# A two-layer fp32 encoder whose instruction order is made with the scheduler's other simulated clock

## The chip, the cores and the metric

The kernel runs on one core of a Trainium2 chip. The metric is the device time of one execution in microseconds (us). The kernel before was run three times: 2852.09, 2852.01 and 2848.87 us, median 2852.01 us. A second set of numbers comes from one execution under the hardware profiler.

## The reference, cut to what matters

Two requests of 512 and 256 tokens, 768 rows in all, share the weights. D is 1024, the hidden width of a feed-forward network (FFN) is 2816, everything is fp32.

```python
def swiglu_ffn(x, w1, w2):
    gate, up = jnp.split(x @ w1, 2, axis=-1)
    return (jax.nn.silu(gate) * up) @ w2
...
# one layer; DEPTH is 2: layer 0 has the HGRN2 mixer, layer 1 windowed attention
x = x + 0.5 * swiglu_ffn(rmsnorm(x, g0), w1a, w2a)
x = x + mixer(rmsnorm(x, g1))
x = x + 0.5 * swiglu_ffn(rmsnorm(x, g2), w1b, w2b)
...
y = rmsnorm(x, final_g)
```

The HGRN2 mixer is a gated linear recurrence in both directions over 8 heads of width 128 (`S_t = diag(f_t) S_{t-1} + k_t v_t^T`). The attention mixer has 16 query and 4 key heads of width 64, a window of 128 tokens to either side, rotary positions on part of a head, and a sink logit for each head.

## The kernel before, in words

**Arithmetic.** Every fp32 operand of a large product is split in two fp32r parts, hi by a cast on ACT and lo by a subtraction on DVE. A product is then three matmuls on PE (hi by hi, hi by lo, lo by hi: `mm3`, lines 261 to 263). Weights are loaded by SP (`load_next`), split by `plain_steps` (lines 166 and 167) or by `quad_steps` (lines 199 and 200), and stand in 8 buffers `w`. There are 8 PSUM banks (`ps`) and 21 large slots (`big`).

**The FFNs** (f0 to f3, one before and one after each mixer) multiply in a Strassen-Winograd form, 7 products p1 to p7 in place of 8. `up_pair` makes a gate tile and an up tile (matmuls on line 421, evacuations on lines 438 to 455). After every four such pairs `down_quad` multiplies by w2: in the order p1, p2, p5, p4, p7, p6, p3 (`DOWN`), each product three banks of 6 matmuls with 512 columns (line 479). A bank of p1 is first added to the residual x (line 501, DVE), then p2 accumulates into the same bank and is added again; p4 does so upon p5, p3 upon p7. So the first matmul of p2 waits for DVE's addition of p1, and the first of p4 for that of p5. This change from up to down happens five times in each FFN, 20 times in all.

**The HGRN mixer.** `hgrn_proj` projects the next head (lines 261 to 263, evacuated on line 654) while `hgrn_scan` goes through the seven levels of a head's scan. A level is six 128 by 128 matmuls (line 671; the trace shows 12 records for them), whose result DVE copies under a mask (line 690); then DVE multiplies q by the level's decay (line 713) and ACT copies the next level's k operand (line 696). The next level's matmuls read that q and that operand, so a level can't start until the one before has gone through DVE. `weave` sets pieces of the next head's projection between the levels.

**The attention mixer.** A unit is a group of four query heads by one block of 128 queries (24 units). `turn` transposes q (line 910) and ACT copies it out (line 1097); `scores` multiplies by k (lines 1106, 1107); then exponentials, a multiplication on POOL (line 1138), the transposes of the probabilities (line 1144), the products with v (lines 1156, 1157), and the split of the outcome (lines 983, 984). `pipeline` sorts all these calls by a step number, with the pieces of the q projection and of the output projection as further events.

**The start and the end.** `load_x` normalizes the first three blocks (lines 303 to 306), turns them (line 323), then starts f0; `up_plain` makes the first tiles (lines 412, 413). `final_block` normalizes and stores each block (lines 1030 to 1037) as soon as f3 has added to it.

**What sets the order.** No engine's order is written out by hand. The code's own order gives each instruction a priority; the Tile framework simulates the program, with a clock for every engine, and puts next on an engine, of the instructions that its simulated clock finds ready, the one that comes first in the code. Pools of buffers, semaphores and waits follow from that order. `kernel` makes the context in line 1277, `with _tile.TileContext(nc) as tc:`; the loops that say what is computed do not depend on it.

## Time and profile before

| | |
|---|---|
| three runs, us | 2852.09, 2852.01, 2848.87 |
| the profiled execution's own time, us | 2852.12 |
| its span in the trace, us | 2850.3 |
| PE busy, us | 2796.7 (98%) |
| DVE busy, us | 2173.2 (76%) |
| ACT busy, us | 1318.9 (46%) |
| POOL busy, us | 355.1 (12%) |

The page gives busy times by engine and the costliest groups; the windows view gives busy times of a stretch, with the clock that was granted to PE; the waits view gives, for each line, how long an engine stood idle and what ended it; the timeline gives single instructions. The stages lie so: the start up to 28 us, f0 until about 540, HGRN until about 1080, f1 and f2 until about 2060, attention until about 2350, f3 and the final norm to the end. An engine carries out its instructions in order, so an instruction that waits holds up what stands behind it.

### The profile page before, as it was taken

What the parts mean: (1) busy time and instruction counts of PE and PEld (TensorE: products, weight loads), DVE (VectorE), ACT (ScalarE), POOL (GpSimd) and SP (SyncE); (2) the same over time, 40 slices, a digit from 0 to 9 for tenths busy, and PEclk for the clock granted to TensorE, in tenths of its full rate; (3) what the DMA queues carried; (4) which work ended last, traced back from release to release, by engine and by line L of the source; (5) the groups of instructions that cost most, each with busy time, mean ns of one, the idle gap of its engine ahead of it and who ended that gap; (6) DMA issues with size and microseconds to landing.
All of it is one profiled execution on the core that took longest, in us unless ns stands there. A gap on an engine that the chain in (4) does not pass through costs nothing. (4 is left out here: it accounts for less than half of the span.)

```text
span 2850.3 us, 40558 instructions
## 1 busy us (share of the span) xinstructions
PE 2796.7 (98%) x15225; PEld 2554.2 (90%) x15225; DVE 2173.2 (76%) x3750; ACT 1318.9 (46%) x2454; POOL 355.1 (12%) x402
## 2 busy tenths in 40 slices
PE   8999999999999999999999999999999899999998
PEld 8899999889899889998998998999888789989997
DVE  7788787468577658878878887887848878788877
ACT  7344443434344336434444643444458755434443
POOL 1111111000000001111111111111002211111110
PEclk9999999999999999999999999999999999999999
DMA  6554454311111133555444355545422113555443
GB/s 165 127 125 122 116 134 121 115 44 39 44 39 38 60 97 86 132 127 122 123 119 114 84 134 127 122 121 124 126 71 75 37 51 90 135 126 125 117 121 96
DMA packets 330101, 291.37 MB, mean 102 GB/s; under 512 B 11608, under 2 KB 257840, under 8 KB 329904
## 3 DMA queue, kind: packets, MB, share of 16 engines
q1 hardware_dynamic: 294064, 212.43, 25.4%
q0 software_dynamic: 31680, 62.93, 12.6%
q10 hardware_dynamic: 4160, 13.42, 1.3%
q8 instruction: 119, 1.95, 0.3%
q14 instruction: 78, 0.64, 0.1%
HBM read 216.39 MB, written 9.44 MB: 79 GB/s over the span
## 5 line engine op out<-in xcount | busy, mean ns | idle before, releaser
L421 PE MATMUL ps<-big,w 128*128 128x384 f32 x6720 | 1172.8, 334 | 3.1 <-DVE tA L444 2.9
L421 PEld LDWEIGHTS ps<-big,w 128*128 128x128 f32 x6720 | 1165.4, 188 | 8.8 <-DVE tA L444 7.2
L199 ACT CAST w<-wr 128x512 fp32r<-128x512 f32 x600 | 416.1, 707 | 722.7 <-PE ps L421 321.0
L479 PE MATMUL ps<-w,big 128*128 128x512 f32 x2520 | 586.8, 391 | 17.4 <-DVE x L501 17.4
L479 PEld LDWEIGHTS ps<-w,big 128*128 128x128 f32 x2520 | 469.4, 188 | 129.7 <-DVE x L501 17.3
L200 DVE TENSOR_TENSOR w<-wr,w 128x512 fp32r<-128x512 f32 (+1 forms) x520 | 438.1, 853 | 95.7 <-ACT w L199 87.0
L501 DVE SCALAR_TENSOR_TENSOR x<-ps,x 128x512 f32<-128x512 f32 x468 | 305.5, 682 | 20.5 <-PE ps L479 10.2
L141 POOL DMA_DIRECT2D s<-wr x120 | 105.4, 878 | 1333.4 <-DMA wr<-in_ffn_w_dram 583.0
L261 PE MATMUL ps<-w,big 128*128 128x512 f32 x624 | 249.8, 400 | 0.2
L263 PE MATMUL ps<-w,big 128*128 128x512 f32 x624 | 245.2, 393 | 2.5 <-DVE big L330 1.3
L262 PE MATMUL ps<-w,big 128*128 128x512 f32 x624 | 244.4, 392 | 0.0
L266 ACT CAST big<-tA 128x384 fp32r<-128x384 f32 x296 | 148.0, 513 | 175.0 <-DVE tA L449 72.0
L261 PE MATMUL ps<-big,w 128*128 128x384 f32 (+2 forms) x640 | 220.8, 346 | 3.3 <-ACT big L266 2.0
L262 PE MATMUL ps<-big,w 128*128 128x384 f32 (+2 forms) x640 | 216.8, 339 | 0.7 <-DVE big L267 0.5
L263 PE MATMUL ps<-big,w 128*128 128x384 f32 (+2 forms) x640 | 215.7, 337 | 0.0
L167 DVE TENSOR_TENSOR w<-wr,w 128x1024 fp32r<-128x1024 f32 x92 | 111.6, 1222 | 83.6 <-ACT w L166 59.7
L141 POOL DMA_DIRECT2D wr<-wr x100 | 87.5, 875 | 680.0 <-DVE tA L350 319.8
L267 DVE TENSOR_TENSOR big<-tA,big 128x384 fp32r<-128x384 f32 x296 | 164.2, 566 | 7.9 <-ACT big L266 4.4
L206 DVE TENSOR_TENSOR wr<-wr,wr 128x512 f32<-128x512 f32 (+1 forms) x100 | 79.3, 793 | 114.5 <-DMA wr<-wr 85.9
L166 ACT CAST w<-wr 128x1024 fp32r<-128x1024 f32 x92 | 96.6, 1052 | 120.5 <-PE ps L262 99.7
L263 PEld LDWEIGHTS ps<-w,big 128*128 128x128 f32 x624 | 117.4, 188 | 28.8 <-DVE big L330 2.0
L261 PEld LDWEIGHTS ps<-w,big 128*128 128x128 f32 x624 | 117.8, 189 | 22.3 <-issue 0.6
(170 smaller groups left out, 3317.2 us busy)
## 6 DMA issues: line engine op xcount, KB each, us to landing
wr<-in_ffn_w_dram SPq DMA_DIRECT2D x264, 512.0 KB, 3.9
s<-in_ffn_w_dram SPq DMA_DIRECT2D x120, 256.0 KB, 3.0
s<-wr POOLq DMA_DIRECT2D x120, 256.0 KB, 4.0
wr<-wr POOLq DMA_DIRECT2D x80, 256.0 KB, 4.0
wr<-in_hg_w_in_dram SPq DMA_DIRECT2D x40, 512.0 KB, 3.8
wr<-wr POOLq DMA_DIRECT2D x20, 512.0 KB, 4.6
spill<-x ACTq DMA_DIRECT2D x12, 512.0 KB, 3.0
x<-spill ACTq DMA_DIRECT2D x12, 512.0 KB, 3.3
```

The lines of the kernel that those rows point to most:

```text
L141: self.nc.gpsimd.dma_start(out, src, accum_op=ALU.add)
L167: self.nc.vector.tensor_sub(lo, raw, hi.bitcast(F32))
L199: nc.scalar.copy(h, src)
L200: (eng or nc.vector).tensor_sub(l, src, h.bitcast(F32))
L261: nc.tensor.matmul(out, a[0], b[0], start=first, stop=False)
L262: nc.tensor.matmul(out, a[0], b[1], start=False, stop=False)
L263: nc.tensor.matmul(out, a[1], b[0], start=False, stop=last)
L266: self.nc.scalar.copy(hi, src)
L267: self.nc.vector.tensor_sub(lo, src, hi.bitcast(F32))
L421: self.nc.tensor.matmul(ps, a[x], b[y], start=first and k == 0 and i == 0, stop=k == 3 and i == 2, skip_group_check=True,)
L479: nc.tensor.matmul(ps, a[x], w[y], start=name == chain and kp == 0 and q == 0, stop=kp == 1 and q == 2, skip_group_check=True,)
L501: self.nc.vector.scalar_tensor_tensor(x, ps, c, x, ALU.mult, ALU.add)
```

## The change

One argument is added where the context is made. The scheduler then takes the time of its simulation from another clock, one that models the timeline of the engines and of their queues. No loop, tile, pool or instruction of the program is edited.

```diff
-    with _tile.TileContext(nc) as tc:
+    with _tile.TileContext(nc, schedule_with_timeline_sim=True) as tc:
         tile_trunk_kernel(tc, *args)
```

Each engine gets the same instructions in another order, but for three activation table loads fewer on ACT (19 for 22; two at the start, around the first use of line 412, and one where the HGRN stage begins). On PE an instruction moves 6 rows on average, at most 61 up and 32 down; on DVE 1.8 rows; POOL's order is the same, and on SP four rows at the start move.

**From up to down in an FFN, on PE (third group of f1).** `ps_11106` is the bank of the last up product p3, `ps_11239` to `ps_11255` are the three banks of p1 and p2 of the down products (weights `w_11122`, `w_11123` for p1, `w_11153`, `w_11154` for p2), `ps_11294` to `ps_11310` those of p5. Before, from the end of p1 to p5:

```order
L479 MATMUL ps_11255<-w_11123,big_10795 128x512
L479 MATMUL ps_11255<-w_11122,big_10795 128x512
L479 MATMUL ps_11239<-w_11153,big_10923 128x512
L479 MATMUL ps_11239<-w_11154,big_10923 128x512
L479 MATMUL ps_11239<-w_11153,big_10923 128x512 x2
```

Now, at the beginning of p1:

```order
L479 MATMUL ps_11239<-w_11122,big_10795 128x512 x2
L479 MATMUL ps_11239<-w_11123,big_10795 128x512
L421 MATMUL ps_11106<-big_9142,w_11064 128x384 x6
L421 MATMUL ps_11106<-big_9145,w_11064 128x384 x6
L479 MATMUL ps_11239<-w_11122,big_10795 128x512
```

And now from the end of p1 on, down to the first matmul of p2:

```order
L479 MATMUL ps_11255<-w_11122,big_10795 128x512
L479 MATMUL ps_11294<-w_11184,big_10951 128x512
L479 MATMUL ps_11294<-w_11185,big_10951 128x512
L479 MATMUL ps_11294<-w_11184,big_10951 128x512
L479 MATMUL ps_11302<-w_11184,big_10951 128x512
L479 MATMUL ps_11302<-w_11185,big_10951 128x512
L479 MATMUL ps_11302<-w_11184,big_10951 128x512
L479 MATMUL ps_11310<-w_11184,big_10951 128x512
L479 MATMUL ps_11310<-w_11185,big_10951 128x512
L479 MATMUL ps_11310<-w_11184,big_10951 128x512
L479 MATMUL ps_11239<-w_11153,big_10923 128x512
```

Five of p1's matmuls now stand ahead of the 12 of the last up product, and nine matmuls of p5 stand between p1 and p2. Further on, pieces of p7 stand between those of p2, and p4 comes after p6's first two banks. The other 19 changes from up to down read alike, but for the lengths of the pieces.

**Two levels of a scan, on PE (first head).** `ps_5321` and `ps_5322` are one level's banks, `ps_5355` and `ps_5356` the next one's; `ps_5313` and `ps_5369` are projection. Before, the level stands so, and 18 matmuls onto `ps_5313` follow before the next level comes:

```order
L262 MATMUL ps_5313<-big_4591,w_5049 128x512
L263 MATMUL ps_5313<-big_4591,w_5050 128x512
L671 MATMUL ps_5321<-big_4938,big_5151 128x128 x4
L671 MATMUL ps_5322<-big_4938,big_5151 128x128 x2
L261 MATMUL ps_5313<-big_4592,w_5049 128x512
L262 MATMUL ps_5313<-big_4592,w_5049 128x512
L263 MATMUL ps_5313<-big_4592,w_5050 128x512
```

Now:

```order
L262 MATMUL ps_5313<-big_4597,w_5049 128x512
L263 MATMUL ps_5313<-big_4597,w_5050 128x512
L671 MATMUL ps_5321<-big_4938,big_5151 128x128 x4
L671 MATMUL ps_5322<-big_4938,big_5151 128x128 x2
L671 MATMUL ps_5355<-big_4938,big_5151 128x128 x4
L671 MATMUL ps_5356<-big_4938,big_5151 128x128 x2
L261 MATMUL ps_5369<-big_4590,w_5049 128x256
```

The 18 projection matmuls have moved ahead of the first of the two levels, and nothing stands between the levels. Eight pairs of levels of the stage stand so now, one in six of the heads and two in one, and one more pair has only four matmuls between; before, the shortest piece between two levels was seven matmuls of 512 columns. On DVE the rows between two such levels are what they were: the two of line 690, line 713, then lines 719 and 717.

**A unit of attention, on PE.** `ps_18983` takes the turned queries, `tA_18988` their copy on ACT, `ps_19003` the first scores; `ps_18889` is output projection. Before:

```order
L910 MATMUL ps_18983<-ident_r,big_18955 128x128 x4
L1144 MATMUL ps_18990<-ident_r,big_18831 128x128 x4
L261 MATMUL ps_18889<-w_18809,big_17852 128x512
L262 MATMUL ps_18889<-w_18810,big_17852 128x512
L263 MATMUL ps_18889<-w_18809,big_17852 128x512
L1106 MATMUL ps_19003<-big_17939,tA_18988 128x256
```

Now:

```order
L1157 MATMUL ps_18936<-tA_18915,big_17943 128x512
L910 MATMUL ps_18983<-ident_r,big_18955 128x128 x4
L1144 MATMUL ps_18990<-ident_r,big_18831 128x128 x4
L1106 MATMUL ps_19003<-big_17939,tA_18988 128x256
L1107 MATMUL ps_19003<-big_17939,tA_18988 128x256
```

The three projection matmuls stand earlier, together with others, in pieces of 12 to 24. Between a unit's turn and its scores there are now at most four transposes of line 1144 in 16 of the 24 units; before it was so in 7.

**The start and the end.** At the start ACT casts two pieces of weights (line 166) earlier, and the table load of line 412 comes after the third square root of line 304. On DVE line 413 now stands ahead of the three of line 306; before it stood behind two of them. At the end the last 72 matmuls of f3 are mixed so that the first block is complete after 27 of them instead of 15, and DVE's last additions of line 501 stand ahead of the multiplications of line 1037.

## The prediction

> **What bounds the kernel now.** I read the page's first part, then the windows of the stages, then the waits of PE, and at last the timeline where the change moves PE's rows. The page:

> ```profile
> span 2850.3 us, 40558 instructions
> PE 2796.7 (98%) x15225; PEld 2554.2 (90%) x15225; DVE 2173.2 (76%) x3750; ACT 1318.9 (46%) x2454; POOL 355.1 (12%) x402
> ```

> PE is busy for all but 2850.3 - 2796.7 = 53.6 us. The change adds and removes no matmul, so at an unchanged pace no more than these 53.6 us can be won, and a loss shows as more of them. The windows tell where they lie (columns: length, busy time of PE, PEld, DVE, ACT, POOL with counts, granted clock, DMA share, GB/s):

> ```profile
> 0.00:50.00 50.00, 37.93 (x211) 36.56 (x212) 35.14 (x50) 39.10 (x66) 5.60 (x10) 0.97 0.67 182
> 600.00:1050.00 450.00, 449.94 (x2778) 402.33 (x2777) 303.69 (x538) 169.89 (x297) 0.00 (x0) 1.00 0.17 50
> 1100.00:2050.00 950.00, 940.00 (x4979) 877.25 (x4978) 766.78 (x1216) 416.24 (x731) 147.87 (x146) 1.00 0.49 121
> 2050.00:2350.00 300.00, 289.42 (x1549) 239.79 (x1548) 214.56 (x597) 203.73 (x513) 53.03 (x98) 0.99 0.20 61
> 2800.00:2850.00 50.00, 42.41 (x223) 39.22 (x221) 33.89 (x56) 20.10 (x38) 1.81 (x1) 0.96 0.22 84
> ```

> In HGRN (600 to 1050) PE idles 0.06 us in 450: nothing can be won there. In f1 and f2 it idles 10.0 us in 950, in attention 10.6 in 300, at the start 12.1 and at the end 7.6. PE's waits (line that waits, what ends the wait: us, times, longest):

> ```profile
> PE ps L479 <- DVE x L501: 17.4, 37, 0.5
> PE ps L910 <- DVE big L267: 3.1, 3, 1.9
> PE ps L421 <- DVE tA L444: 2.9, 5, 1.1
> PE ps L1106 <- ACT tA L1097: 2.5, 6, 1.3
> PE ps L1144 <- POOL big L1138: 2.1, 3, 1.3
> ```

> So the FFNs lose nearly all they lose in one place, where p2 and p4 wait for line 501.

> **Part 1, up to down (20 places).** One place of f1 on PE, then DVE there:

> ```profile
> 1401.79 4.28 PE L479 MATMUL ps<-w,big 128*128 128x512 f32 x18
> 1406.62 10.24 PE L479 MATMUL ps<-w,big 128*128 128x512 f32 x44 [0.54 <-DVE x L501]
> 1417.32 14.80 PE L479 MATMUL ps<-w,big 128*128 128x512 f32 x64 [0.46 <-DVE x L501]
> ...
> 1405.32 0.55 DVE L453 TENSOR_TENSOR tA<-tA,ps 128x384 f32<-128x384 f32 x1
> 1405.79 0.68 DVE L501 SCALAR_TENSOR_TENSOR x<-ps,x 128x512 f32<-128x512 f32 x1
> ```

> A matmul of 512 columns costs 14.80 / 64 = 0.23 us. p1's first bank is full 6 x 0.23 = 1.4 us after 1401.79; DVE, still at the last up product (line 453), adds it only from 1405.79 to 1406.47. p2 would start after 18 matmuls, at 1405.9, and waits until 1406.62. In the new order the last up product's 12 matmuls come five matmuls (1.15 us) later, so that line's work and the addition shift by 1.15 us, to 1407.6; the nine of p5 push p2's start by 9 x 0.23 = 2.1 us, to about 1408.0. The wait goes, with 0.4 us to spare. p4 now follows p6 and most of p7, so its wait for p5's additions should go too; a hand replay leaves between 0 and 0.27 us there. The five waits of line 421 for line 444 (2.9 us) stand at the last up product, which now comes behind five matmuls (1.15 us, the longest wait is 1.1). All of it is 17.4 + 2.9 = 20.3 us; with 20 x 0.27 = 5.4 left, 14.9. I take **-15 us**, between -20 and -8 (the margin of 0.4 us lost in half of the places, 0.54 each, and some left at p4).

> **Part 2, two scan levels back to back (HGRN).** Two consecutive levels of one head:

> ```profile
> 594.85 1.60 PE L671 MATMUL ps<-big,big 128*128 128x128 f32 x12
> 596.20 0.49 PE L261 MATMUL ps<-big,w 128*128 128x512 f32 x1
> 596.01 1.06 DVE L690 COPY_PREDICATED big<-big,ps 128x512 f32<-128x512 uint8 x2 [0.17 <-PE ps L671]
> 596.97 0.94 DVE L713 TENSOR_TENSOR big<-big,big 128x768 f32<-128x768 f32 x1
> 599.03 1.50 PE L671 MATMUL ps<-big,big 128*128 128x128 f32 x12
> 600.29 0.48 PE L261 MATMUL ps<-big,w 128*128 128x512 f32 x1
> 601.08 0.95 DVE L713 TENSOR_TENSOR big<-big,big 128x768 f32<-128x768 f32 x1
> ```

> The level begins at 594.85 and PE is at the next row at 596.20. The following level needs line 713, over at 596.97 + 0.94 = 597.91. Projection covers the 1.71 us between; for the second level it is 602.03 - 600.29 = 1.74. Where nothing stands between, PE must wait those 1.7 us, since the projection taken out has already run: PE was never idle here, so running it sooner wins nothing. Eight pairs at 1.7 make 13.6; the pair with four matmuls (0.91 us) left waits 0.8. Together **+14.4 us**. From below it is 8, if DVE reaches both lines 0.7 us earlier in a quiet stretch; from above 20, if a cast's subtraction (line 167) gets between in some.

> [...]

> ```profile
> 2232.71 0.33 PE L1144 MATMUL ps<-ident_r,big 128*128 128x128 f32 x1 [1.27 <-POOL big L1138]
> 2233.95 0.33 PE L1144 MATMUL ps<-ident_r,big 128*128 128x128 f32 x1 [0.68 <-POOL big L1138]
> 2232.00:2236.00 4.00, 2.61 (x9) 1.91 (x10) 4.00 (x11) 2.66 (x7) 1.89 (x2) 0.82 0.44 132
> 2236.00:2240.00 4.00, 2.91 (x14) 2.10 (x12) 1.72 (x3) 1.81 (x6) 0.00 (x0) 0.76 0.26 73
> ```

> After waits of 1.27 and 0.68 us in quick succession the granted clock was 0.82 and then 0.76 over 8 us. That pair cost 4 x (0.18 + 0.24) = 1.7 us on top. In HGRN each new gap stands alone, several microseconds of matmuls from the next, so I count no clock loss there and keep it as a rival.

> **Part 3, attention.** The turn, its copy and its scores:

> ```profile
> 2226.80 0.46 PE L910 MATMUL ps<-ident_r,big 128*128 128x128 f32 x4
> 2227.47 0.48 PE L261 MATMUL ps<-w,big 128*128 128x512 f32 x1
> 2227.70 0.57 ACT L1097 CAST tA<-ps 128x512 fp32r<-128x512 f32 x1
> 2228.32 0.39 PE L1106 MATMUL ps<-big,tA 128*128 128x256 f32 x1
> ```

> From the turn to the end of the copy it is 2228.27 - 2226.80 = 1.47 us, of which turn and transposes take 0.67. With the projection moved away PE waits up to 0.8 us there. This holds in 16 units instead of 7. The seven cost 2.5 us in six waits, 0.42 each; nine more at that price are +3.8, and if all 16 cost 0.8 it is 12.8 - 2.5 = +10.3. Against it, bundles of 12 to 24 matmuls elsewhere may cover the waits of lines 910 and 1144 (3.1 + 2.1): at best 3.8 - 5.2 = -1.4. I take **+5**, between -2 and +11: nearer the middle of the two, since POOL's and DVE's chains that lines 1144 and 910 wait for are not shortened.

> **Part 4, start and end.** The start:

> ```profile
> 24.22 0.75 DVE L306 TENSOR_SCALAR big<-x,stat 128x1024 f32<-128x1024 f32 x1
> 25.43 1.03 PE L323 MATMUL ps<-ident_r,big 128*128 128x128 f32 x8
> 25.13 0.49 ACT L412 ACTIVATE tA<-ps 128x384 f32<-128x384 f32 x1
> 25.64 1.28 ACT L304 ACT_TABLE_LOAD   x1
> 26.93 0.29 ACT L304 ACTIVATE stat<-stat,eps 128x1 f32<-128x1 f32 x1
> 27.13 1.98 ACT L166 CAST w<-wr 128x1024 fp32r<-128x1024 f32 x2
> 27.10 0.55 DVE L413 TENSOR_TENSOR tA<-tA,ps 128x384 f32<-128x384 f32 x1 [1.40 <-PE ps L263]
> 28.21 0.44 PE L261 MATMUL ps<-big,w 128*128 128x384 f32 x1 [1.23 <-ACT w L166]
> ```

> Two table loads fewer save ACT 2 x 1.28 = 2.6 us, and the wait of 1.23 us for line 166 should go, since that cast is earlier. But line 306, which the turns (line 323) need, now stands behind line 413 on DVE, and that one waits for line 412. ACT now has the two casts (1.98) and a third square root (0.29, the one at 26.93) ahead of line 412's table load: from 23.83, where the load began, it would begin at 26.1, and line 412 end at 26.1 + 1.28 + 0.49 = 27.9. Lines 413 and 306 take 0.55 + 0.75, so the first turn starts near 29.2. PE's other matmuls, which ended at 28.21 - 1.23 = 27.0 with eight turns (1.03) among them, are through at about 26.0: some 3 us of wait for the 1.2 that goes. The start is **+2**, between 0 and +4. At the end the first block is complete 12 matmuls (2.7 us) later, the last matmul stays where it is, and the last additions come sooner on DVE; the norms of six blocks are squeezed into less time. I take **+1.5**, between 0 and +3.

> **The sum.** -15 + 14.4 + 5 + 2 + 1.5 = +7.9 us. The profiled execution took 2852.12 us (its span and 1.8 us around it), the median of the runs is 2852.01, so nothing is to be corrected: 2852.1 + 7.9 = **2860 us**.

> **The rivals.**

> *No change.* The waits between levels are mostly shorter than 1.7 us, about 1.0 (8 + 0.4 us), and attention comes out even: -15 + 8.4 + 0 + 3.5 = -3, 2849 us. For it: the page shows DVE busy 76%, so at some of the pairs it may be ahead of where the two quoted levels caught it. Against it: on DVE the chain is 1.06 + 0.94 = 2.0 us of work however free it is.

> *Faster.* The gaps between levels don't appear at all, because the next level's q is ready when PE comes there; the rest stays: 2852.1 - 6.5 = 2845.6, say 2846 us. It decides from a price of 0.1 us a pair down (8 x 0.1 = 0.8, so that the sum passes -5.7). For it: PE's time in HGRN has been free of waits until now. Against it: both quoted levels give 1.7 us by DVE's rows alone, and DVE's order between the levels is unchanged.

> *Slower still, by the clock.* Each of the nine new gaps brings the clock down as at 2232: 9 x 1.7 = 15 us more, 2875 us. The row for it is that one alone, and it had two gaps within two microseconds. [...]

> That the order would not change is excluded: the rows shown above differ.

> **How the numbers follow.** About 0.2% (5.7 us) is what a measurement of this kernel can tell from no change. My forecast, 2860 us with its own range of 2853 to 2868, has 0.50, no change 0.26, faster 0.12, the clock 0.12. The low end of the forecast's own range, under 2857.8, I set against the high end of the no-change case above it, and leave the cases as they are: slower by over 0.2% 0.50 + 0.12 = 0.62, within 0.2% 0.26, faster 0.12. The range goes from 2845, where the faster rival lies, to 2874, just short of the clock's 2875.

> **What would show it.** Right: PE's wait for line 501 falls from 17.4 us to under 6; line 671 shows about nine waits for line 713 of 1.5 to 1.9 us, and PE idles some 14 us in the HGRN stage, which had 0.06; line 1106 waits more than 2.5 us in all; the clock stays at 1.00 in HGRN. Wrong: part 1 if line 479 still waits for line 501 over 10 us; part 2 if line 671 shows no waits, or if they are of another size; part 3 if attention's idle time falls from 10.6 us; and the whole forecast if the pace of the matmuls changes where PE doesn't wait, since all terms are waits.

## The result, and the profile after

The changed kernel takes 2884.55 us (median of 4 runs, 2882.04 to 2885.64) against 2851.95 for the kernel before (4 runs, 2848.87 to 2852.09). The ratio is 1.0116, with a 95% interval of 1.0098 to 1.0133: slower by 32.6 us, where the forecast was 8 us, and above the range's 2874. The profiled execution took 2884.88 us. Its page and its windows, in the columns of before:

```profile
span 2883.1 us, 40670 instructions
PE 2802.3 (97%) x15225; PEld 2576.1 (89%) x15225; DVE 2158.9 (75%) x3750; ACT 1315.2 (46%) x2451; POOL 369.6 (13%) x402
```

```profile
0.00:50.00 50.00, 36.52 (x194) 35.22 (x195) 28.46 (x43) 31.52 (x56) 4.53 (x9) 0.93 0.69 181
600.00:1050.00 450.00, 432.57 (x2680) 388.10 (x2679) 293.73 (x527) 164.99 (x293) 0.00 (x0) 1.00 0.16 48
1100.00:2050.00 950.00, 947.25 (x5046) 893.04 (x5046) 770.50 (x1230) 426.39 (x746) 155.75 (x146) 1.00 0.48 120
2050.00:2350.00 300.00, 269.64 (x1410) 224.54 (x1409) 199.38 (x569) 187.36 (x482) 51.76 (x96) 0.95 0.18 59
```

PE now idles 17.4 us in HGRN, where it had 0.06, and 30.4 us in the attention window, where it had 10.6; there the granted clock fell to 0.95 too. In the window of f1 and f2 its idle time went from 10.0 to 2.8 us. PE's waits:

```profile
PE ps L671 <- DVE big L713: 13.9, 8, 2.4
PE ps L1106 <- ACT tA L1097: 13.2, 11, 2.3
PE ps L111 <- DMA tB<-in_hg_g_norm_dram: 7.9, 1, 7.9
PE ps L910 <- DVE big L267: 6.6, 2, 4.2
PE ps L261 <- ACT big L266: 5.8, 4, 2.5
PE ps L671 <- ACT big L696: 4.6, 6, 1.7
PE ps L910 <- DVE stat L1134: 3.3, 1, 3.3
```

Line 479's waits for line 501, 17.4 us before, are gone, and so are those of line 421. Windows at fixed times compare different work once one kernel runs behind the other. The following table goes by work: each row is the time from the start of one matmul to the start of another in PE's timeline (FFNs: first to last of line 421, four sums; scan: first to last of line 671; attention: first of line 910 to last of line 1157; seams: what lies between). The cuts don't hold quite the same work: 27 projection matmuls of the seam behind attention now lie in the attention stretch, and six more in the scan.

| stretch, us | before | changed | difference |
|---|---|---|---|
| start, to the first up pair | 55.3 | 58.3 | +3.0 |
| the four FFNs | 1772.3 | 1737.9 | -34.4 |
| seam f0 to scan | 88.1 | 90.9 | +2.8 |
| scan | 363.5 | 384.3 | +20.8 |
| seams scan to f1, f2 to attention | 189.8 | 191.2 | +1.4 |
| seam f1 to f2 | 55.8 | 61.6 | +5.8 |
| attention | 228.7 | 263.3 | +34.5 |
| seam attention to f3 | 72.3 | 69.1 | -3.2 |
| end, from f3's last up product | 24.6 | 26.6 | +2.1 |
| span | 2850.3 | 2883.1 | +32.8 |

One change from up to down in f1, on PE:

```profile
1411.70 1.31 PE L479 MATMUL ps<-w,big 128*128 128x512 f32 x5
1412.86 2.27 PE L421 MATMUL ps<-big,w 128*128 128x384 f32 x12
1414.96 27.63 PE L479 MATMUL ps<-w,big 128*128 128x512 f32 x121
1442.43 37.80 PE L421 MATMUL ps<-big,w 128*128 128x384 f32 x217
```

No wait stands in it: 121 matmuls run through at 27.63 / 121 = 0.228 us. Two scan levels back to back, PE and then DVE:

```profile
607.79 1.50 PE L671 MATMUL ps<-big,big 128*128 128x128 f32 x12
610.93 1.58 PE L671 MATMUL ps<-big,big 128*128 128x128 f32 x12 [1.63 <-DVE big L713]
...
608.88 1.05 DVE L690 COPY_PREDICATED big<-big,ps 128x512 f32<-128x512 uint8 x2 [1.02 <-PE ps L671]
609.83 0.95 DVE L713 TENSOR_TENSOR big<-big,big 128x768 f32<-128x768 f32 x1
```

This is the wait that was forecast, 1.63 us for 1.7: line 713 ends at 610.78, and the level starts 0.15 later. A unit of attention, PE and ACT, and the window that follows:

```profile
2180.70 0.46 PE L910 MATMUL ps<-ident_r,big 128*128 128x128 f32 x4
2180.99 0.62 PE L1144 MATMUL ps<-ident_r,big 128*128 128x128 f32 x4
2183.70 0.39 PE L1106 MATMUL ps<-big,tA 128*128 128x256 f32 x1 [2.08 <-ACT tA L1097]
...
2181.99 0.51 ACT L1122 ACTIVATE big<-big,stat 128x256 f32<-128x256 f32 x1
2182.49 0.50 ACT L1122 ACTIVATE big<-big,stat 128x256 f32<-128x256 f32 x1
2183.07 0.57 ACT L1097 CAST tA<-ps 128x512 fp32r<-128x512 f32 x1
```

```profile
2183.90:2187.50 3.60, 3.60 (x15) 3.13 (x15) 3.30 (x15) 2.61 (x9) 1.71 (x4) 0.53 0.01 3
2201.00:2204.60 3.60, 3.60 (x12) 3.06 (x11) 2.77 (x12) 2.60 (x9) 1.27 (x3) 0.53 0.00 0
```

The copy of the turned queries (line 1097) doesn't start 0.9 us after the turn as in the row of before, but 2.4 us after it, behind the exponentials (line 1122) in ACT's order; PE waits 2.08 us, and for the next 3.4 us the clock is at half. By the trace's record of the clock there are eight such stretches of 3.4 us in the stage, against one before. (The text on the change said that 16 units have at most four transposes between turn and scores; nine have at most four, and 16 have at most six matmuls of any kind, as seven had before.)

### The profile page after: what moved, and what is told of

Same layout as the page of the kernel before. It is cut to its first block, busy times and chain, and to the rows that moved or that the text cites. A ratio compares the mean times of both kernels' runs of the same rounds, so it can differ in the third digit from the quotient of the medians.

```text
span 2883.1 us, 40670 instructions
## 1 busy us (share of the span) xinstructions
PE 2802.3 (97%) x15225; PEld 2576.1 (89%) x15225; DVE 2158.9 (75%) x3750; ACT 1315.2 (46%) x2451; POOL 369.6 (13%) x402
## 4 chain that ended last, share of the span: by engine, by line
PE 93%; ACT 3%; DVE 3%; issue 1%; DMA 0%; POOL 0%; DVEq 0%; SPq 0%; ACTq 0%; POOLq 0%
PE ps L421 40%; PE ps L479 20%; PE ps L261 8%; PE ps L262 8%; PE ps L263 8%; PE ps L671 3%; PE ps L765 1%; PE ps L1144 1%; PE ps L323 1%; ACT big L303 1%; PE ps L1106 0%; DVE x L501 0%; PE ps L1107 0%; DVE w L167 0%; PE ps L1157 0%
## 5 line engine op out<-in xcount | busy, mean ns | idle before, releaser
L421 PE MATMUL ps<-big,w 128*128 128x384 f32 x6720 | 1172.7, 334 | 0.0
L421 PEld LDWEIGHTS ps<-big,w 128*128 128x128 f32 x6720 | 1167.0, 188 | 3.1
L479 PE MATMUL ps<-w,big 128*128 128x512 f32 x2520 | 579.0, 389 | 0.0
L479 PEld LDWEIGHTS ps<-w,big 128*128 128x128 f32 x2520 | 472.4, 188 | 96.7 <-DVE x L501 0.4
L501 DVE SCALAR_TENSOR_TENSOR x<-ps,x 128x512 f32<-128x512 f32 x468 | 300.6, 681 | 10.3 <-PE ps L263 10.3
L261 PE MATMUL ps<-w,big 128*128 128x512 f32 x624 | 250.0, 401 | 3.9 <-DVE big L330 3.9
L263 PE MATMUL ps<-w,big 128*128 128x512 f32 x624 | 245.8, 397 | 0.0
L261 PE MATMUL ps<-big,w 128*128 128x384 f32 (+2 forms) x640 | 221.1, 348 | 5.8 <-ACT big L266 5.8
L263 PE MATMUL ps<-big,w 128*128 128x384 f32 (+2 forms) x640 | 217.2, 340 | 0.0
L267 DVE TENSOR_TENSOR big<-tA,big 128x384 fp32r<-128x384 f32 x296 | 178.6, 620 | 26.4 <-ACT big L266 26.2
L200 POOL TENSOR_TENSOR w<-wr,w 128x512 fp32r<-128x512 f32 x80 | 134.5, 1681 | 201.1 <-ACT w L199 201.1
L166 ACT CAST w<-wr 128x1024 fp32r<-128x1024 f32 x92 | 97.0, 1056 | 104.3 <-PE ps L262 87.5
L261 PEld LDWEIGHTS ps<-w,big 128*128 128x128 f32 x624 | 119.2, 191 | 26.2 <-DVE big L330 4.4
```

The lines of the kernel that those rows point to most:

```text
L200: (eng or nc.vector).tensor_sub(l, src, h.bitcast(F32))
L261: nc.tensor.matmul(out, a[0], b[0], start=first, stop=False)
L263: nc.tensor.matmul(out, a[1], b[0], start=False, stop=last)
L267: self.nc.vector.tensor_sub(lo, src, hi.bitcast(F32))
L421: self.nc.tensor.matmul(ps, a[x], b[y], start=first and k == 0 and i == 0, stop=k == 3 and i == 2, skip_group_check=True,)
L479: nc.tensor.matmul(ps, a[x], w[y], start=name == chain and kp == 0 and q == 0, stop=kp == 1 and q == 2, skip_group_check=True,)
```

## The experiments

All hold an engine's order by edges that ask for issue order alone, with no wait. Every instruction stays, but for the twelfth, which adds some. The medians are of 4 runs (10 for the third); the kernel before took 2849.8 to 2851.5 us beside them.

| kernel | us | ratio to before, interval | FFNs | scan | attention |
|---|---|---|---|---|---|
| before | 2851.95 | | 1772.3 | 363.5 | 228.7 |
| changed | 2884.55 | 1.0116 (1.0098 to 1.0133) | 1737.9 | 384.3 | 263.3 |
| e1_scan_pin | 2866.68 | 1.0056 (1.0041 to 1.0071) | 1737.5 | 365.8 | 263.2 |
| e2_attn_pin | 2865.81 | 1.0051 (1.0036 to 1.0066) | 1737.6 | 384.0 | 245.0 |
| e3_both_pin | 2845.82 | 0.9983 (0.9973 to 0.9992) | 1737.5 | 365.9 | 242.3 |
| e4_down_pin | 2988.17 | 1.0481 (1.0464 to 1.0499) | 1843.1 | 384.4 | 267.0 |
| e5_pe_before | 2949.92 | 1.0345 (1.0328 to 1.0363) | 1854.4 | 364.7 | 234.0 |
| e6_mix_before | 2837.04 | 0.9951 (0.9936 to 0.9966) | 1738.8 | 364.8 | 233.9 |
| e7_ffn_after | 2834.65 | 0.9945 (0.9930 to 0.9959) | 1754.6 | 363.5 | 229.0 |
| e8_pe_after | 2892.08 | 1.0145 (1.0129 to 1.0162) | 1754.9 | 384.7 | 254.8 |
| e9_rest_before | 2820.56 | 0.9891 (0.9876 to 0.9906) | 1737.8 | 365.1 | 229.1 |
| e10_ffn_pe_dve | 2833.07 | 0.9938 (0.9923 to 0.9953) | 1752.0 | 365.1 | 230.1 |
| e11_ffn_pe_act | 2818.99 | 0.9889 (0.9872 to 0.9905) | 1737.6 | 364.9 | 227.5 |
| e12_fill | 2880.77 | 1.0103 (1.0088 to 1.0118) | 1737.5 | 384.3 | 261.6 |

**PE held to the order of the code, stretch by stretch (e1 to e4).** The edit in the scan; e2 does it around `self.pipeline(...)`, e3 both, e4 around the down products of each group:

```diff
-        lead = 4
+        lead, since = 4, mark(self)
...
-        self.drain(g0)
+        self.drain(g0), pin(self, since)
...
+def pin(k, since):
+    pe = [i for i in traced[: first + 1] if i.engine == mybir.EngineType.PE][-1:]
+    pe += [i for i in traced[first + 1 :] if i.engine == mybir.EngineType.PE]
+    for a, b in zip(pe, pe[1:]):
+        k.tc.add_manual_dep(b, a.name, dep, reason="pin")
```

e1, expected: 

> The changed program, with PE alone held to the order of the code from the first scan level to the last, which is within a few rows the order before; ACT and DVE stay free. Theory (PE's order between levels makes the loss): line 671's waits for line 713 go, the stretch from the first level's matmul to the last goes from 384.3 us back to about 363.5, the time from 2884.6 to about 2864. Rival (ACT's and DVE's new order delays the levels by itself): more than half of the 20.8 us stays, 2874 or more.

The scan went from 384.3 to 365.8 us, line 671's waits for line 713 are gone, and the time fell by 17.9 us. The loss in the scan is PE's order.

e2, expected: 

> The changed program, with PE alone held to the order of the code in the attention units. Theory (the projection that was taken from between turn and scores makes the loss, idle time and lowered clock alike): line 1106's waits fall from 13.2 us to under 4, the lowered clock in the stage goes from eight windows of 3.4 us to one or two, the stretch from the first turn to the last product with v goes from 263.3 us to about 230, the time from 2884.6 to about 2851. Rival (ACT and DVE reach the copies and splits later by their own new order): at least half stays, 2867 or more.

Line 1106's waits fell to 3.2 us and four of the eight lowered stretches of the clock are gone, but attention came down only to 245.0 us, by 18.3 of 34.5. In numbers the rival's value, 2867, is the nearer one. The code's order is not quite that of before in this stage, so the run doesn't tell yet what the rest is. Its waits in the stage:

```profile
PE ps L910 <- DVE big L267: 8.0, 6, 3.7
PE ps L1144 <- POOL big L1138: 4.3, 5, 1.8
PE ps L1106 <- ACT tA L1097: 3.2, 9, 0.5
```

e3, expected: 

> Both stretches held at once. Theory (the two losses are independent and the gain of the FFNs stays): 2884.6 - 20.8 - 33 = about 2831 us, faster than the kernel before by 21. Rival (the gain in the FFNs and the loss in the mixers are one, as weights or buffers come later): above 2845.

The two add up (-17.9 and -18.7 make -36.6; measured -38.7) and the FFNs keep their gain, so the losses are independent as the theory had it. The number, 2845.8, lies in the rival's range all the same, since e2 gave back 18.3 us of attention and not 33. It is 0.2% below the kernel before.

e4, expected: 

> The changed program, with PE alone held to the order of the code through the down products of the FFNs (last up product first, then p1, p2, p5, p4 and so on), the scheduler's clock as changed. Theory A (the gain of 34.4 us in the four FFNs comes from this order, and each wait costs 0.16 us more than its listed idle time, as the listing takes a matmul's end 0.39 us after its start where the pace is 0.23): some 37 waits for line 501 are back with 17 us listed, and the time rises by 23 to 34 us, to 2908 to 2919. Theory B (the listed idle time is the whole price): it rises by 17 to 20, to 2902 to 2905. Theory C (the gain comes from the up pairs' order or from DVE's): under 2895.

It rose by 104 us, far outside all three. The new waits stand in each of the 20 groups after 39 down matmuls, which are the 36 of p1 and p2 and the first three of p5: there p5 waits for the split of its operand (line 479 for line 267: 36.7 us, for line 266: 17.9 us). The order of the code is not quite that of before (in the code p4 follows p5 at once, while before eight matmuls of p7 stood ahead of it), but p5 follows p2 in both, and e5 below has the same waits with the exact order of before. So the new orders of ACT and DVE prepare p5's operand too late for a PE that goes from p2 to p5 without a piece between.

**PE's whole order, row by row (e5 to e8).** The runs of the order are written into the kernel, for all matmuls or for those in or outside the FFNs; e5 and e6 are built with the new clock, e7 and e8 with the old one:

```diff
-    k.ffn("f3", None)
+    k.ffn("f3", None); pin(k)
...
+def pin(k):
+    runs = [int(n) for n in RUNS.split()]
+    pe = [pe[n] for a, c in zip(runs[::2], runs[1::2]) for n in range(a, a + c)]
+    for a, b in zip(pe, pe[1:]):
+        k.tc.add_manual_dep(b, a.name, dep, reason="pin")
```

e5, expected: 

> The scheduler's clock as changed, PE held row by row to the order that it had before; ACT and DVE keep the order that the new clock gives them (ACT's rows stand 5.0 away from before on average, DVE's 1.0). Theory (PE's order alone makes the difference): the time of before, 2851 us, within 5; line 501's waits are back with about 17 us. Rival (ACT's order costs by itself, at the start and at the changes of stage): 2858 or more.

2949.92 us, 98 more than before with the very same order on PE. The FFNs lost 82 us. One change from up to down:

```profile
1438.89 4.28 PE L479 MATMUL ps<-w,big 128*128 128x512 f32 x18
1443.41 5.02 PE L479 MATMUL ps<-w,big 128*128 128x512 f32 x21 [0.24 <-DVE x L501]
1449.34 0.73 PE L479 MATMUL ps<-w,big 128*128 128x512 f32 x2 [0.90 <-ACT big L266]
1451.93 21.02 PE L479 MATMUL ps<-w,big 128*128 128x512 f32 x85 [1.86 <-DVE big L267]
```

The theory fell, and the rival is right in its number alone, since the loss is not at the start or the changes of stage. As in e4 it is p5's operand that comes through ACT and DVE later than PE's old order asks for it (18 + 21 matmuls, then the two waits; in all groups 17.8 us for line 266 and 37.3 for line 267, close to e4's). The granted clock of the run also fell, to 0.982 from 0.998. The four FFNs' gain is not PE's alone; the orders of the engines belong together.

e6, expected: 

> The scheduler's clock as changed; PE is held to its order of before everywhere except in the four FFNs, where it keeps the new order. Theory (the FFNs' gain of 34.4 us is their own, and all losses are PE's order elsewhere): 2851 - 34 = 2817 us, faster than both kernels. Rival (ACT's new order costs at the start and at the changes of stage, where the run with both mixers held still lost 3 to 6 us each): 2825 to 2832.

The FFNs kept 1738.8, the scan and attention came back to 364.8 and 233.9. The time is 2837.0, past the rival's end: ACT's and DVE's new order alone costs some 19 us outside the FFNs (5.1 of them in attention, 3.5 at the seam after it, 2.4 at the seam from f1 to f2; from the stretches of the two traces).

e7, expected: 

> The kernel before with its own scheduler's clock, PE held in the four FFNs to the order of the changed program and free elsewhere (where it stays row by row what it was); ACT and DVE stay within half a row of before. Theory A (the new order of PE alone makes the gain, and the gain is the 34.4 us by which the four FFNs became shorter): 2851 - 34 = 2817. Theory B (only the idle time that the waits list, 17.4 + 2.9 us, can go): 2831. Theory C (the gain hangs on ACT's or DVE's new order): 2840 or more.

FFNs 1754.6, time 2834.65. PE's order alone brings 17.7 of the 34.4 us; line 501's waits fall from 17.4 to 8.9 us. They also move: before, they stood at p2 (17 of 37) and p4 (20), and now 14 of 17 stand at the 56th down matmul of a group, the first onto the third bank of p7. Theory B came nearest in the number, but e11 below shows that its ground, listed idle time as the most that can go, is wrong.

e8, expected: 

> The kernel before with its own scheduler's clock, PE held everywhere, row by row, to the order of the changed program; ACT and DVE are free under the old clock. Theory (PE's order alone): 2884 us as the changed kernel, within 5. Rival (ACT's and DVE's new order costs too): 2875 or less.

2892.08 us: the scan lost 21.2 us as in the changed kernel, attention 26.1 of 34.5, the FFNs gained 17.4. The time lies above both expectations, because the FFNs' second half is missing. ACT was free here and moved along (it has 19 table loads, as in the changed kernel, and not the 22 of before), so the 26.1 us are those of PE's order with what the old clock makes of ACT behind it. Its longest waits:

```profile
PE ps L671 <- DVE big L713: 13.3, 8, 1.9
PE ps L910 <- DVE big L267: 9.9, 4, 3.4
PE ps L1106 <- ACT tA L1097: 9.7, 10, 1.6
PE ps L479 <- DVE x L501: 9.1, 17, 0.7
```

**Which engine makes the second half (e9 to e11).** The same `pin`, for several engines, each with its own runs:

```diff
+    for engine, text in RUNS.items():
+        all_ = [i for i in traced if str(i.engine) == "EngineType." + engine]
+        runs = [int(n) for n in text.split()]
+        row = [all_[n] for a, c in zip(runs[::2], runs[1::2]) for n in range(a, a + c)]
```

e9, expected: 

> The scheduler's clock as changed; outside the four FFNs PE, DVE and ACT are all held to their order of before, inside they keep the new one. Theory (the FFNs' gain is made by PE's, DVE's and ACT's new order together, and outside nothing is lost once all three stand as before): the FFNs last 1738 us as in the changed kernel instead of 1772, the rest as before, 2850 - 34 = 2816 to 2819 us, the fastest so far. Rival (the seams between the two orders cost what is won): 2827 or more.

2820.56 us: the FFNs' gain is whole, and the rest costs what it cost before.

e10, expected: 

> The kernel before with its own clock; in the FFNs PE and DVE are held to the order of the changed program, ACT is free. With PE alone so held the FFNs lasted 1754.6 us, 17.7 less than before and 16.7 more than changed. Theory (DVE's new order, which adds a finished bank sooner, makes the second half): FFNs 1738 to 1741 us, 2817 to 2821 in all. Rival (ACT's order makes it): about 2834 as with PE alone.

FFNs 1752.0: DVE's order adds 2.6 us to PE's. The theory fell. Line 501's listed waits did fall further, from 8.9 to 3.4 us, but those of line 421 for line 444 rose from 0.9 to 1.8.

e11, expected: 

> The same with PE and ACT held to the order of the changed program in the FFNs, DVE free. Theory (DVE makes the second half): 2832 to 2837 us, FFNs about 1754, line 501's waits 9 us as with PE alone. Rival (ACT makes it): 2817 to 2821, FFNs about 1738.

FFNs 1737.6 and 2818.99 us, 1.1% below the kernel before; with e9, from which its interval doesn't part it, the fastest. The rival was right: it is ACT's order. Rows of the same change from up to down, first with PE's order alone (e7), then with ACT's too (e11):

```profile
1288.50 1.64 ACT L199 CAST w<-wr 128x512 fp32r<-128x512 f32 x3
1289.90 1.99 SPq L151 DMA_DIRECT2D wr<-in_ffn_w_dram  x2
1301.43 1.05 ACT L199 CAST w<-wr 128x1024 fp32r<-128x1024 f32 x1 [1.28 <-DMA wr<-wr]
1301.49 1.23 DVE L206 TENSOR_TENSOR wr<-wr,wr 128x1024 f32<-128x1024 f32 x1 [5.85 <-DMA wr<-wr]
1303.81 1.32 PE L479 MATMUL ps<-w,big 128*128 128x512 f32 x5
...
1311.23 0.69 DVE L501 SCALAR_TENSOR_TENSOR x<-ps,x 128x512 f32<-128x512 f32 x1
1318.53 0.69 DVE L501 SCALAR_TENSOR_TENSOR x<-ps,x 128x512 f32<-128x512 f32 x1
1319.27 0.97 PE L479 MATMUL ps<-w,big 128*128 128x512 f32 x3 [0.64 <-DVE x L501]
```

```profile
1281.18 0.61 ACT L199 CAST w<-wr 128x512 fp32r<-128x512 f32 x1
1283.05 3.47 SPq L151 DMA_DIRECT2D wr<-in_ffn_w_dram  x2
1295.22 1.04 ACT L199 CAST w<-wr 128x1024 fp32r<-128x1024 f32 x1
1295.22 1.23 DVE L206 TENSOR_TENSOR wr<-wr,wr 128x1024 f32<-128x1024 f32 x1 [4.82 <-DMA wr<-wr]
1298.97 1.32 PE L479 MATMUL ps<-w,big 128*128 128x512 f32 x5
...
1302.23 13.12 PE L479 MATMUL ps<-w,big 128*128 128x512 f32 x57
...
1304.96 0.69 DVE L501 SCALAR_TENSOR_TENSOR x<-ps,x 128x512 f32<-128x512 f32 x1
1309.44 0.69 DVE L501 SCALAR_TENSOR_TENSOR x<-ps,x 128x512 f32<-128x512 f32 x1
```

All times are counted from p1's first matmul. DVE's first addition comes after 5.99 us instead of 7.42, and its work ahead of that addition (from line 206 on) starts when a DMA of weights lands, 3.75 us ahead instead of 2.32: the same 1.43 us. ACT's cast just ahead of p1 waits for that DMA too (1.28 us in e7), so that cast is not the lever. The trace leads back to earlier casts: the first cast of the weights before these starts 17.79 us ahead instead of 15.31, the subtraction on DVE (line 200) that follows it gives the buffer free, and SP's next load, which waits for that subtraction, goes out 15.92 us ahead instead of 13.91. The wait of 0.64 us is that of p7's third bank: p1, p5 and p7 hold three banks each, nine where the kernel has eight, so one must be given free by the addition of p2's first bank, which starts after 10.47 us instead of 14.72. That ACT's order is the lever is what the runs show; the way from cast to addition is read from this one place.

**PE kept busy in attention's waits (e12).** PE's real matmuls keep the changed kernel's order, and ACT and DVE too; six matmuls are added ahead of the first scores of 16 units and then overwritten:

```diff
+        for _ in range(6):
+            r = u.k.nc.tensor.matmul(ps, u.k.identr, u.kT[:, 0, u.keys], start=True, stop=True)
...
-        nc.tensor.matmul(ps, qi, self.kT[:, 0, self.keys], start=True, stop=False)
+        fill(self, i, ps); nc.tensor.matmul(ps, qi, self.kT[:, 0, self.keys], start=True, stop=False)
```

Expected: 

> The changed program with every real instruction in its place, and six matmuls more (0.7 to 1.0 us) ahead of the first scores in the 16 attention units that have next to nothing between turn and scores; they write the scores' own bank, which the scores then overwrite, and need nothing that is late. They don't shorten any chain, they only keep PE at work in its waits. Theory (part of attention's loss is the clock, lowered for 3.4 us after gaps of about 2 us, at 1.7 us each): of the eight lowered windows in the stage at least four go, line 1106's waits fall from 13.2 us to under 5, and the stretch from the first turn to the last product gets shorter, from 263.3 to 254 to 260 us, though 96 matmuls were added. Rival (the gaps themselves are the loss, the clock falls without a price): 263 to 268, since some of the added matmuls find no gap.

Four of the eight lowered stretches went, line 1106's waits fell from 13.2 to 6.5 us, and attention took 261.6 us: shorter, though less so than expected. The 96 matmuls are 13.8 us of work (0.13 us each with 256 columns, 0.174 with 384). All listed waits of the stage together fell by 5.6 us (28.3 to 22.6), so 8.2 us of the work found no listed wait. That the stage became 1.7 us shorter all the same leaves 9.9 us; four stretches at 1.7, which half speed over 3.4 us comes to, make 6.8 of them, and the rest stays open. The price shows better in the seam behind, whose two waits are the same in both (0.45 and 1.19 us): the lowered stretch at 2385 of the changed kernel is absent here, and the seam takes 67.6 us instead of 69.1. The added matmuls have no part in that, as they all stand in the stage.

## Why the prediction was wrong

**The direction and two mechanisms were right, two sizes were not, and errors of both signs met.** By its terms:

*Part 1, up to down, forecast -15, measured -34.4.* The waits are gone, but the price was mis-sized twice. First, the waits view counts from a matmul's modelled end, 0.39 us after its start, while matmuls follow at 0.227. The prediction's own row held this: p2 should start at 1405.88 (18 matmuls at 0.227) and started at 1406.62, 0.74 us lost of which 0.54 are listed. In f1 before, matmuls start late in 22 places by 8.7 us together, and the gaps behind modelled ends make 5.6 of them; in the changed kernel both are zero. Second, the step took ACT as it was, and replayed p2 and p4 alone. With ACT as it was, 8.9 us of line 501's waits stay (e7), nearly all of them at the third bank of p7, which the replay did not look at. ACT's new order is worth 17 of the 34.4 us (e7 and e11); with PE's order alone the term would have been -17.7, near the forecast for a wrong reason.

*Part 2, scan levels, forecast +14.4, measured +20.8.* Mechanism, places and price were right: seven pairs wait 1.63 us for 1.7, the eighth 2.42, the pair with four matmuls between 0.72 for 0.8; 14.6 us in all. (At the last of these line 713 ended 0.06 us ahead of an ACT copy, line 851, to which the profile puts the wait down.) Five small waits for the k operand (line 696, 2.9 us in the scan) were not counted. The last 3.3 us no listed wait shows: six more projection matmuls lie in the stretch (1.4 us), and the lowered clock at 965.6 (0.50 for 3.4 us) slows the last level, which takes 2.80 us instead of 1.5. e1 takes 18.5 us back.

*Part 3, attention, forecast +5 with an end at +11, measured +34.5.* This is the step that failed. It priced the projection that was taken away by line 1106's waits alone, at no more than 0.8 us each by one row in which the copy started 0.9 us after the turn; it let the waits of lines 910 and 1144 at best shrink; and it put the clock at nothing. The runs showed three things in its place. First, in the kernel before the copy already started up to 1.64 us after the turn, in units where the projection covered it (and one listed wait was 1.3); in the changed kernel, in the units that wait, it starts up to 2.6 us after the turn, and the longest of the 11 waits took 2.3 us. Line 1106's waits rose by 10.6 us. Second, the other listed waits of the stage rose too, by 8.7 us, lines 910 and 1144 from 5.3 to 11.1: 9.0 to 28.3 us in all, by 19.3. Third, there are seven more lowered stretches of the clock, at up to 1.7 us each 11.9 more. The 27 projection matmuls that came into the stretch from the seam behind are 6.1 us of work that was no loss. These make 37.3 at most for 34.5 measured; how they share exactly stays open. PE's order makes most of it: 26.1 us come with it under the old clock (e8), and with PE's old order under the new clock only 5.2 are left (e5).

*Part 4.* The start was +3.0 for +2 (in e1, e2, e3 and e12, which leave it as it is, it was +1.0 to +2.8): line 412's table load began at 25.89 (forecast 26.1) and the turn at 29.08 (29.2). The end was +2.1 for +1.5. Not forecast at all are the seams, +6.8 together, of which +5.8 between f1 and f2: there PE waits 2.53 us for a split (line 266), and the clock is lowered for 6.8 us.

*The clock rival* was placed wrongly. In the scan the granted clock stayed at 1.00 through all gaps of 1.63 us; it fell in attention. That a gap which stands alone costs no clock was the author's estimate: it held for these seven gaps, but not for the one of 2.42 us at the end of the scan, behind which the clock fell (0.50 from 965.6 to 969). In attention all five gaps of 1.96 to 2.35 us had a lowered stretch begin within 1.5 us, and a gap of 3.33 us at 2154.97 had none, so the length of a gap alone doesn't price this kernel.

*The other rivals* are out: the gaps between levels did appear, and gains and losses did not cancel.

## What to carry to other kernels

When a scheduler reorders, follow the engine that feeds the wait as closely as the one that waits: here PE's rows were replayed, and ACT's were taken as they had been, which left out half of the FFNs' gain, and one copy stood for all 24 units, which hid most of attention's loss. Price a wait by starts at the known pace, since the listed idle time of pipelined matmuls left part of a wait out here (at 1406.62 of the kernel before, 0.74 us lost and 0.54 listed). A program-wide scheduling choice can be good for one stage and bad for another: kept for PE and ACT in the FFNs alone, this one gives 2818.99 us instead of 2884.55.

## What the runs showed of the hardware

```profile
2130.00:2170.00 40.00, 34.33 (x190) 28.71 (x188) 25.66 (x85) 27.68 (x70) 6.38 (x12) 1.00 0.17 53
2170.00:2210.00 40.00, 34.62 (x176) 28.86 (x176) 24.18 (x83) 22.97 (x65) 11.86 (x24) 0.91 0.13 40
```

The gap of 3.33 us lies in the first, and the clock stays at 1.00. Those of 2.08 us (ahead of 2183.70) and 2.29 us (ahead of 2199.94) lie in the second; a lowered stretch began 0.43 us after the one and 1.26 us after the other. In the attention stretch 96 added matmuls that are thrown away made the time 1.7 us shorter and not longer (261.6 for 263.3, one execution each); the medians of the whole kernel, 2880.77 and 2884.55 us, have ranges that touch.
